# Weaving the fourth retention head with the last delta-rule pair in a two-layer encoder trunk

## The chip, the cores and the metric

The kernel runs on one core of one Trainium2 chip. The metric is the device time of one launch in microseconds (us). The core has a matrix engine (PE, whose weight loads are listed apart as PEld), a vector engine (DVE), a scalar engine (ACT), GpSimd (POOL) and a queue engine that issues the DMAs (SP).

## What is computed

Sixteen learned tokens and 512 input tokens (528 rows of 1024) pass two layers. Each layer adds a token mixer and then a gated feed-forward block; a last norm follows, and the 16 tokens are dropped. The token mixer has two branches that read the same normed input:

```python
o_a = o_fwd + o_bwd            # gated delta rule, 8 heads of 128, both directions
o_a = rms(o_a) * gdn_gain * silu(z_a);  y_a = o_a @ w_up_a
o_b = rms(r_fwd + r_bwd)       # retention, 4 heads, keys of 256, values of 512
o_b = o_b * silu(g_b);          y_b = o_b @ w_up_b
merged = sigmoid(gate_a) * y_a + sigmoid(gate_b) * y_b
return merged @ w_out
```

The delta rule runs chunk by chunk: in each chunk of 128 tokens a triangular system is solved, and a state of 128 x 128 is carried from chunk to chunk. Retention has no state here: scores of all token pairs are formed and weighted by a decay.

## The kernel before

Activations lie transposed, 128 channels by 528 tokens. Products that need fp32 accuracy are made of three passes: a weight tile is split into a high and a low part (`whi`, cast on ACT, L178; `wlo`, on DVE, L179), the activations likewise (`xh`, `xl`), and each of the 8 steps of the contraction issues three matmuls (`mmps`). One projection of 128 output channels is a **unit**. In layer 0 a unit is two halves of 264 tokens, 48 matmuls; in the last layer only 512 tokens are needed for most outputs, and a unit is 24 matmuls of 512 columns, but units for keys and values keep 48. A unit's raw weights (512 KB) come by one DMA into one of three buffers, the split parts into four.

In each layer the eight delta-rule heads run as four pairs (`gi` 0 to 3). `gdn_begin` projects a pair. `gdn_chain` is the long dependent part: products, a solve of about 30 dependent DVE steps that goes out to DRAM (`xd`) and comes back, two rounds of block levels (matmuls `lvy`, `lvt`, `lvq`, `l`, `l64b`), a scan of five chunk steps (matmuls `ks`, `yy`, `sn`, `oo`), and `gdn_squares`, which writes the pair's output to DRAM (`od_a`) and appends a mean-square job to the list `later`. A job in `later` is issued by the next call of `sums`: small matmuls (`oms`), an ACT copy (`ms`) and a DMA to `msd`.

`retention(h)` is a generator over the work of one retention head: two units for queries, two for keys, the rotation, a call of `sums`, the units that were handed in as `filler`, five score blocks (`rs`, evacuated to `pr`) with the units of values 0 and gates 0 among them, and then a loop over four value tiles: values (`dv`), `weighted` (matmuls `rpv`), gates. `filling` chains retention heads 0 to 2, the z gates and the merge gates up to 13.

`weave(a, na, b, nb)` sets the program order. Every generator yields an estimated cost; the loop advances `b` (the filling) and lets `a` (the chain) keep up in the ratio na to nb, until `b` has yielded nb in sum or is empty; then it issues the rest of `a` in one go. The constants are `NA` 71 and `NB` 86. The yields of a whole chain add up to 85.95 in layer 0 and 83.05 in the last layer, so about 15 units of cost at the end of each chain are issued in one go. In the last pair the filling is empty sooner: adding up the yields by hand, the weave ends with the chain at 53.85, in the levels of the second head, and its remaining 32 (29 in the last layer), the whole scan among them, follow in one go. Then comes `retention(3)` with merge gates 14 and 15, by itself, and a last `sums`.

The program order is a priority and not the order of execution. A planner orders the instructions of each engine ahead of the run: it takes the first instruction whose inputs and buffers it expects to be ready, so later work may be pulled forward. PSUM tiles of projections, score blocks and `oms` of these calls share one tag of four buffers; most temporary tiles share a tag of six.

After the mixer, `load_a` (issued with a high priority) turns the eight mean squares into inverse roots (`ir`), reads back the eight delta outputs and z gates (`lo`, `lz`, `rs`), and makes split tiles (`oh`, `ol`) for the projection with `w_up_a`. `load_b` does so for retention, ahead of `w_up_b`.

Of the kernel before, what the change touches and what calls it, by code (L numbers as in the profile page):

```python
# [33 lines left out]
SW = L + 400  # L34
NA = 71.0
NB = 86.0
GF = 2
G0 = 3
HW = 2
# [360 lines left out]
def layer(tc, nc, env, l, xn, gd):  # L400
# [233 lines left out]
    def gdn_decayed(h, st):  # L634

        s = st[h]
        for d in range(2):
            gr = s["gr"][d]
            act(gr, gr, AF.Exp)
            tt(gr, gr, s["q"], MUL)  # L640
        act(s["q"][:, t0:L], s["q"][:, t0:L], AF.Square)
        for c in range(NCH):
            n = tok(c)[1]
            vt = s["vtok"][0:n, c]
            act(vt, vt, AF.Copy, scale=st["nk"][0:n, c, h % 2:h % 2 + 1])
        yield 2.2

    def gdn_solve(st):
        w0 = st["w0"]
        w3 = w0.rearrange("p (r i) -> p r i", r=32)  # L650
        nc.gpsimd.memset(w0[:, 0:1024:33], 1.0)
        for q in range(30, 0, -1):
            n = 31 - q
            t = gp.tile([68, 256], F32, name="st", tag="sc", bufs=SB)[:, :q * n].rearrange("p (j i) -> p j i", j=q)
            tt(t, bc(w3[:, 0:q, q:q + 1], [68, q, n]), bc(w3[:, q:q + 1, q + 1:32], [68, q, n]), MUL)
            tt(w3[:, 0:q, q + 1:32], w3[:, 0:q, q + 1:32], t, ADD)
            if q % 2:
                yield 1.05
        xd = dp.tile([68, 1024], F32, name="xd", tag="xd", bufs=2)
        nc.sync.dma_start(xd, w0)  # L660
        st["xd"] = xd
        yield 4.0
# [181 lines left out]
    def gdn_squares(h, st):  # L844

        s = st[h]
        (o, om), q = s["o"], s["q"]
        o = o.rearrange("p c d -> p (c d)")
        nc.sync.dma_start(od_a[h, :, NM:L], o)
        sq = s["k"]  # L850
        act(sq[:, NM:L], o, AF.Square)
        if not last:
            nc.sync.dma_start(od_a[h, :, 0:NM], om)
            act(sq[:, 0:NM], om, AF.Square)
        stt(sq[:, t0:L], q[:, t0:L], 128.0 * 128.0 * EPS, sq[:, t0:L], MUL, ADD)
        hi, lo = (gp.tile([P, L], F32R, name=n, tag="gcr", bufs=4) for n in ("osh", "osl"))
        split(hi[:, t0:L], lo[:, t0:L], sq[:, t0:L])
        later.append(lambda ps: mean_square(h, (hi, lo), 4.0 / 128.0, 4 * 128 * EPS * 4 * EPS, tmp("ms"), ps))
        yield 1.0
# [3 lines left out]
    def sums(ps):  # L863

        while later:
            later.pop(0)(ps)
# [28 lines left out]
    def gdn_chain(gi, st):  # L895
        hs = (2 * gi, 2 * gi + 1)

        nk = gp.tile([P, NCH, 2], F32, name="nk", tag="nk")
        ssv = st["ssk"].rearrange("p h c -> p c h")
        rk = gp.tile([P, NCH, 2], F32, name="rk", tag="rk")  # L900
        ts(rk, ssv, 4 * EPS, ADD)
        rv, nv = (t.rearrange("p c h -> p (c h)") for t in (rk, nk))
        stt(nv, inverse_root(rv, 2 * NCH), 0.5, rv, MUL, MUL)
        nc.vector.reciprocal(rk, rk)
        cc = gp.tile([P, 2, NCH, 2], F32, name="cc", tag="cc")
        cs = gp.tile([P, 2, NCH, 2], F32, name="cs", tag="cs")
        for d in range(2):
            tt(cc[:, d], beta[:, d, :, 2 * gi:2 * gi + 2], rk, MUL)
            tt(cs[:, d], cc[:, d], sS[:, d, :, 2 * gi:2 * gi + 2], MUL)
        cn = gp.tile([P, 2, NCH, 2], F32, name="cn", tag="cn")  # L910
        ts(cn, cc, -1.0, MUL)
        st.update(nk=nk, cc=cc, cs=cs, cn=cn)
        yield 1.0
        for h in hs:
            yield from gdn_products(h, st)
        for h in hs:
            yield from gdn_decayed(h, st)
        yield from gdn_solve(st)
        for h in hs:
            yield from gdn_levels(h, st)  # L920
        yield from gdn_scan(hs, st)
        for h in hs:
            yield from gdn_squares(h, st)
# [9 lines left out]
    def retention(h, filler):  # L933
# [54 lines left out]
        def values(dv):  # L988
            V[dv] = tmp("rvc")

            def consume(t, n0, n, ps):
                nc.scalar.copy(V[dv][:, n0:n0 + n], ps)
            yield from units(W, C_VB + h * DV + dv * P, 1, xn, FULL, consume)

        def gates(dv):
            G[dv] = tmp("rg")
            yield from units(W, C_GB + h * DV + dv * P, 1, xn, tail, gated(G[dv]))

        def turn(dv):

            vc = V[dv]
            rv = rp.tile([P, 2, NC * P], F32R, name="rv", tag="rot", bufs=2)
            vh, vl = rv[:, 0], rv[:, 1]
            vst = vsts[dv % 2]
            ps = pt("rvt")
            for c in range(NC):
                n0, n = tok(c)
                nc.tensor.transpose(ps[:, c * P:(c + 1) * P], vc[:, n0:n0 + n], ident)
            split(vh, vl, ps)
            pm = pt("rvm")  # L1010
            nc.tensor.transpose(pm[0:NM, 0:P], vc[:, 0:NM], ident)
            split(vst[0:NM], vst[64:64 + NM], pm[0:NM, 0:P])
            nc.scalar.copy(vst[32:32 + NM], vst[0:NM].bitcast(F32))
            V[dv] = vh, vl, vst

        def weighted(dv):
            vh, vl, vst = V[dv]
            o = tmp("ro")
            sq = tmp("rsq2") if S else rp.tile([P, SW], F32, name="rsq", tag="strip")[:, 0:L]
            S.append(sq)  # L1020
            for n0, n in tail:
                ps = pt("rpv")
                for c in range(NC):
                    for a, b in ((vh, 0), (vh, 1), (vl, 0)):
                        mm(ps[:, :n], a[:, c * P:(c + 1) * P], pr[c][b][:, n0:n0 + n], start=c + b == 0 and a is vh, stop=False)
                mm(ps[:, :n], vst, pst[:, n0:n0 + n], start=False)
                act(sq[:, n0:n0 + n], ps[:, :n], AF.Square)
                tt(o[:, n0:n0 + n], ps[:, :n], G[dv][:, n0:n0 + n], MUL)
            nc.sync.dma_start(od_b[h * 4 + dv, :, t0:L], o[:, t0:L])
            if dv:  # L1030
                tt(S[0][:, t0:L], S[0][:, t0:L], sq[:, t0:L], ADD)
# [10 lines left out]
        for dv in range(1, 5):  # L1042
            if dv < 4:
                yield from values(dv)
            weighted(dv - 1)
            yield 3.2
            if dv < 4:
                turn(dv)
                yield from gates(dv)
# [4 lines left out]
    def merge_gates(i0, i1):  # L1054

        for i in range(i0, i1):
            th = tmp("mg")

            def consume(t, n0, n, ps):
                act(th[:, n0:n0 + n], ps, AF.Tanh, scale=0.5)  # L1060
            yield from units(W, C_GA + i * P, 1, xn, tail, consume)
            nc.sync.dma_start(gd[i, :, t0:L], th[:, t0:L])

    def units(src, c0, nt, xs, halves, consume):
        for t in range(nt):
            project(src, c0 + t * P, 1, xs, halves, lambda _, n0, n, ps: consume(t, n0, n, ps))
            yield 5.4

    def z_gates(h0, h1):
        for h in range(h0, h1):  # L1070
            z = tmp("z")
            yield from units(W, C_Z + h * P, 1, xn, tail, gated(z))
            nc.sync.dma_start(zd[h, :, t0:L], z[:, t0:L])

    def weave(a, na, b, nb):

        i = j = 0.0
        while j < nb:
            y = next(b, None)
            if y is None:  # L1080
                break
            j += y
            while a is not None and i * nb < j * na:
                x = next(a, None)
                if x is None:
                    a = None
                    break
                i += x
        for x in a or ():
            i += x  # L1090

    def filling():
        for h in range(3):
            yield from retention(h, z_gates(2 * h, 2 * h + 2))
        yield from z_gates(6, 8)
        yield from merge_gates(G0 + 3 * GF, 14)

    fill = filling()
    for gi in range(4):
        st = {}  # L1100
        extra = merge_gates(G0 + GF * (gi - 1), G0 + GF * gi if gi else 0)
        weave(gdn_begin(gi, st), 32.0, extra, GF * 5.4)
        for _ in extra:
            pass
        weave(gdn_chain(gi, st), NA, fill, NB)
    for _ in fill:
        pass
    for _ in retention(3, merge_gates(14, 16)):
        pass
    sums(pt)  # L1110
    mixctx.close()
# [169 lines left out]
    x2, _ = boundary(nrm, hs, lambda xs, two, **kw: first_units([gate(0), up(0), gate(1)], xs, two, **kw))  # L1281
# [88 lines left out]
```

## Time and profile before

| | us |
|---|---|
| median of 3 runs | 2922.13 |
| lowest and highest | 2919.28, 2929.7 |
| profiled execution, its time | 2919.6 |
| span of its trace | 2917.7 |
| PE busy | 2822.1 (97% of the span) |
| DVE busy | 1795.2 (62%) |
| ACT busy | 1101.0 (38%) |
| chain that ended last: PE, DVE, DMA | 84%, 8%, 5% |

Layer 0 fills the first half of the span and layer 1, the last, the second. The part that the change touches, from the last pair's levels to the start of the projection with `w_up_a`, lies between 762 and 907 us and between 2205 and 2351 us. In a table of windows, busy time is summed for each engine, and "PEclk" is the mean granted clock of PE as a share of 2.4 GHz. A matmul whose line ends in brackets was preceded by PE idle time, and the brackets say how long and which instruction ended it.

### The profile page before, as it was taken

Reading aid. Unit: us, or ns where it says so; the run is one execution under the profiler, and the core shown is the slowest. Engines: PE = TensorE matmul, PEld = TensorE weight load, DVE = VectorE, ACT = ScalarE, POOL = GpSimd, SP = SyncE. Lnnn points to the kernel's source line nnn. Section 1 sums busy time; section 2 is a strip of 40 time slices with the busy share of each in tenths; the row PEclk is TensorE's granted clock in tenths of the full one; section 3 lists DMA queues with packets and bytes.
Section 4 is the critical chain, followed back from the end, with each engine's and each line's share of the span. In section 5 each row is a group of like instructions: output and inputs, shape, how many; then the busy total and the mean of one; then the engine's idle time right before and its main releaser. Section 6 shows DMA issues by size and latency. Waiting matters only on the chain.

```text
span 2917.7 us, 48775 instructions
## 1 busy us (share of the span) xinstructions
PE 2822.1 (97%) x19487; PEld 2579.0 (88%) x19487; DVE 1795.2 (62%) x3854; ACT 1101.0 (38%) x2171; POOL 9.0 (0%) x114
## 2 busy tenths in 40 slices
PE   8999999999999999999999999999997999999998
PEld 8999999999889999999999888888886788888887
DVE  6877858768664545343258779687786564543433
ACT  5444445345333233222234344453443332332222
POOL 0000000000000000000000000000000000000000
PEclk9999999999899999999999999999998999999999
DMA  5433323324245442333444423334241464433332
GB/s 166 112 83 83 100 77 85 99 74 125 70 145 171 137 143 84 91 89 99 123 116 112 107 71 108 88 94 106 71 140 44 154 192 125 130 109 94 92 110 80
DMA packets 506423, 313.48 MB, mean 107 GB/s; under 512 B 55633, under 2 KB 460779, under 8 KB 506195
## 3 DMA queue, kind: packets, MB, share of 16 engines
q1 hardware_dynamic: 506194, 310.36, 37.1%
q8 instruction: 153, 2.51, 0.4%
q14 instruction: 76, 0.61, 0.1%
HBM read 265.28 MB, written 45.02 MB: 106 GB/s over the span
## 4 chain that ended last, share of the span: by engine, by line
PE 84%; DVE 8%; DMA 5%; ACT 2%; issue 1%; SPq 0%; DVEq 0%; ACTq 0%
PE mmps L112 67%; PE rpv L112 3%; PE fu L112 2%; PE oo L112 2%; PE sn L112 1%; DVE wlo L179 1%; PE yy L112 1%; DMA xd<-w 1%; PE ks L112 1%; DMA lo<-od_a 1%; PE rs L112 1%; PE lvy L112 1%; PE lvt L112 1%; DMA lo<-od_b 1%; PE lvq L112 1%
## 5 line engine op out<-in xcount | busy, mean ns | idle before, releaser
L112 PE MATMUL mmps<-xh,whi 128*128 128x264 f32 (+1 forms) x3840 | 1188.0, 310 | 23.7 <-DVE rg L115 12.4
L112 PE MATMUL mmps<-xl,whi 128*128 128x264 f32 (+1 forms) x3840 | 1179.5, 308 | 0.0
L112 PE MATMUL mmps<-xh,wlo 128*128 128x264 f32 (+1 forms) x3808 | 1173.3, 308 | 0.0
L112 PEld LDWEIGHTS mmps<-xh,whi 128*128 128x128 f32 x3840 | 727.2, 189 | 63.2 <-DVE rg L115 14.6
L178 ACT CAST whi<-wraw 128x1024 fp32r<-128x1024 f32 (+1 forms) x392 | 407.3, 1040 | 991.2 <-PE mmps L112 737.0
L179 DVE TENSOR_TENSOR wlo<-wraw,whi 128x1024 fp32r<-128x1024 f32 (+1 forms) x392 | 474.4, 1210 | 485.3 <-ACT whi L178 484.4
L112 PEld LDWEIGHTS mmps<-xl,whi 128*128 128x128 f32 x3840 | 726.2, 189 | 37.0 <-issue 2.9
L112 PEld LDWEIGHTS mmps<-xh,wlo 128*128 128x128 f32 x3808 | 719.9, 189 | 34.3 <-issue 0.5
L112 PE MATMUL mmps<-oh,whi 128*128 128x264 f32 (+2 forms) x1126 | 358.5, 319 | 0.0
L112 PE MATMUL mmps<-oh,wlo 128*128 128x264 f32 (+2 forms) x1126 | 358.1, 318 | 0.0
L112 PE MATMUL mmps<-ol,whi 128*128 128x264 f32 (+2 forms) x1126 | 357.3, 318 | 0.5 <-DVE ol L179 0.4
L112 PEld LDWEIGHTS mmps<-ol,whi 128*128 128x128 f32 x1126 | 211.6, 188 | 16.4 <-DVE ol L179 0.9
L112 PEld LDWEIGHTS mmps<-oh,wlo 128*128 128x128 f32 x1126 | 211.7, 188 | 15.7 <-issue 0.2
L112 PEld LDWEIGHTS mmps<-oh,whi 128*128 128x128 f32 x1126 | 211.5, 188 | 15.0
L115 DVE SCALAR_TENSOR_TENSOR ac<-xc,cw,ac 128x528 f32<-128x528 f32 x192 | 143.6, 759 | 3.4 <-ACT ac L125 0.6
L118 DVE TENSOR_TENSOR ff<-fg,mmps 128x264 f32<-128x264 f32 (+1 forms) x63 | 32.5, 516 | 116.0 <-PE mmps L112 116.0
L112 PE MATMUL rpv<-prh,rv 128*128 128x264 f32 (+1 forms) x384 | 95.5, 323 | 0.0
L118 DVE TENSOR_TENSOR st<-w 68x30 f32<-68x30 f32 (+14 forms) x240 | 78.2, 326 | 19.0 <-DMA w<-ndm 7.1
L118 DVE TENSOR_TENSOR w<-w,st 68x30 f32<-68x30 f32 (+14 forms) x240 | 78.2, 326 | 6.8
L125 ACT ACTIVATE gth<-mmps 128x264 f32<-128x264 f32 (+1 forms) x132 | 59.8, 454 | 57.4 <-PE mmps L112 57.4
L112 PE MATMUL rs<-rot 128*128 128x264 f32 (+3 forms) x240 | 75.1, 456 | 2.8 <-DVE z L115 2.4
L115 DVE SCALAR_TENSOR_TENSOR hn<-mmps,hold 128x264 f32<-128x264 f32 (+2 forms) x51 | 25.4, 498 | 82.6 <-PE mmps L112 76.5
(315 smaller groups left out, 3216.3 us busy)
## 6 DMA issues: line engine op xcount, KB each, us to landing
wraw<-in_w_in_dram SPq DMA_DIRECT2D x194, 512.0 KB
wraw<-in_w_ffn_in_dram SPq DMA_DIRECT2D x88, 512.0 KB
wraw<-in_w_up_b_dram SPq DMA_DIRECT2D x32, 512.0 KB
wraw<-in_w_ffn_out_dram SPq DMA_DIRECT2D x32, 512.0 KB
gcr<-grow SPq DMA_DIRECT2D x32, 264.0 KB
wraw<-in_w_up_a_dram SPq DMA_DIRECT2D x16, 512.0 KB
wraw<-in_w_out_dram SPq DMA_DIRECT2D x16, 512.0 KB
wraw<-in_w_ffn_out_dram SPq DMA_DIRECT2D x16, 384.0 KB
```

What stands on the lines that cost most here:

```text
L112: newest[0] = nc.tensor.matmul(o, lhsT=l, rhs=r, start=start, stop=stop)
L115: (eng or nc.vector).scalar_tensor_tensor(out=o, in0=a, scalar=s, in1=b, op0=op0, op1=op1)
L118: (eng or nc.vector).tensor_tensor(out=o, in0=a, in1=b, op=op)
L125: nc.scalar.activation(o, a, f, **kw)
L178: a = nc.scalar.copy(hi, src)
L179: return a.ins, nc.vector.tensor_tensor(out=lo, in0=src, in1=hi.bitcast(F32), op=SUB).ins
```

## The change

The last pair's chain is woven up to 86 instead of 71, with the filling up to 86 x 86 / 71 = 104.2, so the ratio of the two stays. `retention(3)` with merge gates 14 and 15 becomes the end of `filling` instead of a loop of its own after it. And in the loop over value tiles of `retention`, `sums` is called after the values are projected, ahead of `weighted`.

```diff
 NA = 71.0
 NB = 86.0
+NZ = 86.0
...
         for dv in range(1, 5):
             if dv < 4:
                 yield from values(dv)
+            sums(pt)
             weighted(dv - 1)
...
         yield from merge_gates(G0 + 3 * GF, 14)
+        yield from retention(3, merge_gates(14, 16))
...
-        weave(gdn_chain(gi, st), NA, fill, NB)
+        weave(gdn_chain(gi, st), *((NA, fill, NB) if gi < 3 else (NZ, fill, NZ * NB / NA)))
     for _ in fill:
-        pass
-    for _ in retention(3, merge_gates(14, 16)):
         pass
     sums(pt)
```

## Rows read from the trace of the kernel before

**Rows 1.** Head of the page: busy us, share of span, instructions

```profile
PE 2822.1 (97%) x19487; PEld 2579.0 (88%) x19487; DVE 1795.2 (62%) x3854; ACT 1101.0 (38%) x2171; POOL 9.0 (0%) x114
```

**Rows 2.** Windows, layer 1: stretch, length, busy by engine, PEclk, DMA share, GB/s

```profile
2205.00:2215.00 10.00, 0.00 (x0) 0.00 (x0) 5.98 (x13) 4.57 (x14) 0.00 (x0) 0.74 0.36 80
2215.00:2225.00 10.00, 8.71 (x56) 7.76 (x56) 3.24 (x9) 2.29 (x9) 0.00 (x0) 0.57 0.12 22
2225.00:2235.00 10.00, 6.29 (x40) 5.87 (x40) 4.62 (x12) 3.08 (x11) 0.00 (x0) 0.66 0.01 2
...
2257.00:2267.00 10.00, 7.57 (x29) 5.54 (x28) 3.26 (x7) 2.56 (x5) 0.00 (x0) 0.83 0.14 54
...
2294.00:2306.00 12.00, 7.80 (x52) 7.48 (x52) 9.91 (x17) 4.38 (x9) 0.00 (x0) 0.86 0.76 231
...
2205.00:2351.00 146.00, 123.77 (x712) 103.75 (x713) 78.79 (x164) 51.40 (x119) 0.00 (x0) 0.91 0.32 96
```

**Rows 3.** Windows of the same kind, layer 0

```profile
775.00:785.00 10.00, 8.66 (x58) 7.75 (x58) 2.94 (x8) 1.50 (x5) 0.00 (x0) 0.60 0.01 2
785.00:796.00 11.00, 11.00 (x61) 9.99 (x60) 6.41 (x20) 4.25 (x15) 0.00 (x0) 0.69 0.01 1
...
811.00:821.00 10.00, 7.25 (x38) 6.20 (x37) 3.02 (x6) 3.24 (x9) 0.00 (x0) 0.66 0.16 54
...
842.00:862.00 20.00, 16.15 (x115) 13.91 (x116) 18.06 (x30) 9.04 (x18) 0.00 (x0) 1.00 0.87 266
...
762.00:907.00 145.00, 131.83 (x972) 122.46 (x973) 83.85 (x183) 53.70 (x130) 0.00 (x0) 0.92 0.34 101
```

**Rows 4.** Timeline of PE, layer 1: start, us, engine, line, tiles, shape, count

```profile
2204.59 0.39 PE L112 MATMUL oms<-prl,one 128*1 128x512 f32 x1
2215.39 2.08 PE L112 MATMUL lvy<-QT,N 128*128 128x128 f32 x8 [10.42 <-DVE QT L118]
...
2256.96 0.65 PE L112 MATMUL oo<-P,xx 128*128 128x128 f32 x4
...
2260.66 0.39 PE L112 MATMUL mmps<-xh,whi 128*128 128x512 f32 x1
```

**Rows 5.** Timeline of DVE, layer 1, the last weight split before the scan

```profile
2205.51 1.23 DVE L179 TENSOR_TENSOR wlo<-wraw,whi 128x1024 fp32r<-128x1024 f32 x1 [2.96 <-ACT whi L178]
```

**Rows 6.** Timeline of PE, layer 0, around the first level

```profile
763.02 1.16 PE L112 MATMUL lvy<-QT,N 128*128 128x128 f32 x8 [1.43 <-DVE QT L118]
763.93 0.37 PE L112 MATMUL mmps<-xh,whi 128*128 128x264 f32 x1
```

**Rows 7.** Sums of windows over levels and scans, woven pairs, layers 0 and 1

```profile
sum 229.00, PE 224.94 PEld 212.89 DVE 143.33 ACT 92.67 POOL 1.23; mean PE 24.99 PEld 23.65 DVE 15.93 ACT 10.30 POOL 0.14
...
sum 131.50, PE 129.48 PEld 120.46 DVE 86.02 ACT 55.25 POOL 0.77; mean PE 21.58 PEld 20.08 DVE 14.34 ACT 9.21 POOL 0.13
```

**Rows 8.** Timelines, both layers: last oms of the pair, last ol of load_a

```profile
819.84 0.64 PE L112 MATMUL oms<-osl,one 128*1 128x264 f32 x2
...
864.42 0.70 DVE L179 TENSOR_TENSOR ol<-lo,oh 128x528 fp32r<-128x528 f32 x1
...
2266.86 0.39 PE L112 MATMUL oms<-osl,one 128*1 128x512 f32 x1
...
2308.60 0.69 DVE L179 TENSOR_TENSOR ol<-lo,oh 128x512 fp32r<-128x512 f32 x1
```

**Rows 9.** Chain that ended last, both layers: start, us, engine, tile, line, count

```profile
861.98 3.16 PE rpv L112 x26
...
903.95 3.17 PE rpv L112 x26
...
2306.46 3.02 PE rpv L112 x13
...
2342.30 5.57 PE mmps L112 x24
2347.86 3.00 PE rpv L112 x13
```

## The prediction

> **What bounds the kernel now.** I read the page's head first: PE is busy for 97% of the span [rows 1], and no other engine comes near. So only two things can move the time much: PE work that goes away, and PE time in which nothing, or only half as much, is done. The change removes no matmul, so I went on to tables of windows over each layer and looked for stretches where PE busy falls or the granted clock does. Outside the start and the ends of the layers they sit in one place per layer, around the levels and scan of the last pair. In layer 1 PE does nothing at all from 2205 to 2215, and then runs at a mean granted clock of 0.57 and 0.66 for 20 us, between its levels of 1.2 and 2.4 GHz [rows 2]; layer 0 has the same picture, milder [rows 3]. The timeline tells why. The last matmul before the hole ends at 2205.0, and PE stands 10.42 us until the solved blocks come (`lvy`) [rows 4]. Yet the split weights of the next units were there: the last `wlo` before the scan ends at 2206.7 [rows 5], four sets are buffered, and no unit runs until 2260.66, right behind the scan's last `oo` at 2257.6 and the first `oms` [rows 4]. What holds the units is program order: in `retention(3)` the call of `sums` stands ahead of merge gates 14 and 15, it holds the mean squares of the last pair, which wait for the end of the scan, and the units behind it take PSUM tiles of the same tag. That the planner serves a tag in program order is my reading of these rows; it isn't written in the kernel.
>
> **What the lost time is worth.** Idle time is the window less PE busy: 146 - 123.77 = 22.2 us in layer 1 [rows 2] and 145 - 131.83 = 13.2 us in layer 0 [rows 3]. To it comes busy time at a low clock, which I price at busy x (1 - clock). Layer 1: 8.71 x 0.43 + 6.29 x 0.34 + 7.57 x 0.17 + 7.80 x 0.14 = 8.3 us [rows 2]. Layer 0: 8.66 x 0.40 + 11.00 x 0.31 + 7.25 x 0.34 = 9.3 us [rows 3]. Together 53.0 us. The Trainium skill (Perfetto Trace Analysis, Identifying the Most-Contended Engine) warns that matmul busy time is a bad measure and asks for the weight loads' busy time instead. By that the loss would be 146 - 103.75 and 145 - 122.46, together 64.8 us [rows 2, 3]. I don't take it: of the woven stretches in layer 1, where PE has next to no idle time, weight loads fill only 120.46 of 131.5 us [rows 7]; and at the low clock both measures look full, as between 785 and 796 us, where only the clock shows the loss [rows 3].
>
> **The change, part by part.**
> *Order of the last pair.* With the same ratio, nothing moves until the filling is empty, at cost 53.85 of the chain. From there two units of queries and two of keys, merge gates 14 and 15, score blocks 0 and 1 and values 0 come between the rest of the levels and the scan. Those four first units ran before the levels already, in the solve's shadow; what is new is all that stood behind `sums`. That call now finds only the job of retention 2. So merge gates 14 and 15, five score blocks, values 0, gates 0 and values 1 may run as soon as their inputs are there: six units and scores, over 30 us of PE work (a unit is 5.57 us [rows 9]). The holes before the scan's end are smaller than that. For the 10.42 us hole, two units with weights in place make 11.1 us.
> Does the planner see the hole? It can only fill what its own clock shows. In layer 0 it put `lvy` ahead of the last matmuls of the keys, and PE then waited 1.43 us [rows 6]. So its clock for the solve's end was early by about that. I take 1.4 us as the part of a hole it would miss.
> *What stays.* In the other five pairs, where filling was at hand, levels and scan left 229 - 224.94 = 4.1 us idle in three pairs of layer 0 and 131.5 - 129.48 = 2.0 us in the two pairs of layer 1 that I summed [rows 7], so 1.4 and 1.0 us a pair, 2.4 us in both layers. Then the stalls while `load_a` runs: 12 - 7.80 = 4.2 us idle and 1.1 us of low clock in layer 1 [rows 2], 20 - 16.15 = 3.9 us in layer 0 [rows 3]. `load_a` is not removed, it only meets another part of the retention, so I keep them: 9.2 us (bounds 0 to 18: gone, or doubled).
> *The new call of sums.* For pairs 0 to 2 and in the earlier heads `later` is empty there, so it issues nothing. In the last pair it issues the two mean squares, ahead of `weighted(0)`. On PE's queue all of `weighted` and what follows stands behind these `oms`; they wait for the scan's end. In a dense order the scan ends some 20 us before PE has done the work that stands ahead of them, so I cost this wait at nothing. If the chain ran longer than that, PE would stand.
> *DMAs and the other engines.* The moved head issues twelve weight loads of 512 KB on SP, two gate stores, four output stores and one decay strip. They pass the two or four output stores of the pair and its small reads of `xd`. Buffered weights for four units (22 us) cover the time that SP waits for the solve's blocks; if the cover failed, the bound is the 10.42 us hole again. On DVE and ACT the evacuations of scores, values and gates, and a weight split of 1.23 us [rows 5] per unit, now come between the steps of the scan. That makes the chain longer, by between 0 and some 10 us (eight such splits), but PE is what is full there, and this is free so long as `oms` isn't late.
> *What is late next.* `load_a` needs all eight mean squares. From the last `oms` to its last `ol` it took 2309.3 - 2267.3 = 42.0 us in layer 1 and 865.1 - 820.5 = 44.6 in layer 0 [rows 8]. Before, `oms` had nearly the whole head behind it as cover. Now the cover is what follows values 1: from the first `rpv` to the end of the last, 2350.9 - 2306.5 = 44.4 us and 907.1 - 862.0 = 45.1 us [rows 9]. The first unit with `w_up_a` reads the eighth head last, some 4.9 us (7/8 of 5.57) after it starts. So the slack is 44.4 + 4.9 - 42.0 = 7.3 us in layer 1 and 45.1 + 4.9 - 44.6 = 5.4 us in layer 0. It just fits.
>
> **Sum.** 53.0 - 2.4 - 9.2 = 41.4 us: 24.2 in layer 1 (30.5 less 1.0 and 5.3), 17.2 in layer 0 (22.5 less 1.4 and 3.9). The profiled execution took 2919.6 us, so it would take 2878.2. It lies 2.5 us under the median of the runs, and against the median I forecast 2922.1 - 41.4 = **2881 us**. With the bounds of the kept stalls and 1.4 us missed per hole this case spans 2868 to 2893.
>
> **The rivals.**
> *load_a becomes the bound.* Its DVE work now runs against the loop over value tiles, and DVE is an in-order queue that was nearly full while it ran (18.06 of 20 us [rows 3], 9.91 of 12 [rows 2]). If it takes a third longer, or the chain ends as much later, layer 1 loses 14.0 - 7.3 = 6.7 us and layer 0 14.9 - 5.4 = 9.5. With some 4 us of low clock behind such holes the gain is 21 us: **2901**. For it: the slack is thin. Against: the loop loads DVE less than the scores did.
> *The holes stay.* The planner thinks the solve is done sooner than it is, and queues the new work behind `lvy`. Then the 10.42 us hole [rows 4] and the low clock behind it (5.9 us in layer 1 [rows 2]), 1.4 us [rows 6] and 6.9 us in layer 0 [rows 3] remain: 24.6 us less, **2905**. Against it stands the 1.43 us of layer 0, which shows the planner's clock to be nearly right.
> *The clock.* Small matmuls between units leave short gaps, and the clock could swing. The Trainium skill (TensorE: Matmul & The Clock Gate, A second HAM failure mode: psum-queue depth-cycling) says that many micro-idles between groups of matmuls do that. If the stretch from the first level to `oms` (about 67 and 80 us) ran at a mean of 0.75, midway between the levels, it would lose a quarter, some 37 us: **2918**. Against: the woven pairs lost only 1.0 to 1.4 us of idle time each [rows 7], so there are few gaps.
> *Slower.* The same `load_a`, but much later: it needs its inverse roots through DRAM and 24 reads of tiles, and the loop's evacuations and weight splits stand with it on DVE and SP. If it took twice as long, PE would wait 42.0 - 7.3 = 34.7 us in layer 1 and 44.6 - 5.4 = 39.2 in layer 0, and 73.9 - 41.4 = 32.5 us would be lost: **2955**. It decides at (41.4 + 7.3 + 5.4) / 86.6 = 0.62, so from 1.6 times its present length on. Nothing in the rows points to that.
>
> **How the numbers follow.** Forecast 0.64, load_a the bound 0.18, holes stay 0.08, clock 0.05, slower 0.05. About 0.5% (14.6 us) is what a measurement of this kernel can tell from no change. Faster by more: the forecast, the first rival and half of the second (2905 lies at the edge of 2907.5), 0.86. Within: the other half and the clock, 0.09. Slower: 0.05. The range must leave out no more than 2 in 10: the forecast's own 2868 to 2893, widened to the first rival, gives 2866 to 2903.
>
> **What would show it.** Right: `mmps` between 2205 and 2215 and between `lvy` and `lvt`; a granted clock near 1.00 through the last pair; `oms` of the last pair some 20 to 30 us later than before and behind a unit of values; the first `w_up_a` unit some 24 us earlier in layer 1 than 2351. Wrong: `lvy` still waiting 10 us with nothing ahead; a wait of PE for `ol` or `oh` at the first `w_up_a` unit, which means `load_a` ends late; `oms` waiting for `osh`, which means the chain ends late; or units behind `sums` that start only after `oms`, which means the buffers' order wasn't what held them.

## The result and the profile after

The changed kernel takes 2885.28 us (median of 4 runs, 2884.81 to 2888.39); beside it the kernel before took 2925.91 (2919.28 to 2931.21). The ratio is 0.986, with a 95% interval of 0.985 to 0.987: some 40 us less, where 41.4 were forecast; the forecast of 2881 us lies 4 us below the median. The profiled executions lie 34.9 us apart in span (2917.7 and 2882.8), and it is this difference that the parts below add up to. The head of the page of after, which answers [rows 1]:

```profile
span 2882.8 us, 48770 instructions
PE 2809.8 (97%) x19487; PEld 2567.1 (89%) x19487; DVE 1795.3 (62%) x3854; ACT 1099.1 (38%) x2171; POOL 8.9 (0%) x114
```

The instructions are the same in number, on every engine. PE is busy for 12.3 us less (2822.1 - 2809.8); no matmul is gone, and more of them ran at the full clock. The rest of the 34.9, 22.6 us, is idle time that went. Windows of after, with the columns of [rows 2]; the first six are layer 1, the last three layer 0:

```profile
2200.00:2210.00 10.00, 10.00 (x50) 7.39 (x50) 8.58 (x16) 6.31 (x14) 0.00 (x0) 1.00 0.70 188
2210.00:2220.00 10.00, 10.00 (x86) 8.25 (x85) 6.13 (x15) 5.92 (x19) 0.00 (x0) 1.00 0.18 37
2220.00:2230.00 10.00, 10.00 (x44) 6.43 (x44) 5.21 (x8) 3.10 (x6) 0.00 (x0) 1.00 0.22 54
2260.00:2275.00 15.00, 11.63 (x56) 8.85 (x55) 6.78 (x17) 4.85 (x10) 0.00 (x0) 0.89 0.15 54
2275.00:2315.00 40.00, 40.00 (x225) 34.69 (x224) 27.01 (x47) 13.78 (x26) 0.00 (x0) 1.00 0.75 225
2192.00:2315.00 123.00, 118.69 (x721) 98.27 (x719) 75.32 (x161) 49.28 (x116) 0.00 (x0) 0.99 0.40 114
...
820.00:850.00 30.00, 26.03 (x193) 23.32 (x192) 18.36 (x56) 10.28 (x29) 0.00 (x0) 0.94 0.14 46
860.00:870.00 10.00, 7.78 (x51) 7.25 (x50) 8.44 (x14) 4.89 (x11) 0.00 (x0) 0.83 1.07 338
759.00:894.00 135.00, 128.06 (x994) 119.22 (x993) 84.59 (x184) 53.35 (x132) 0.00 (x0) 0.97 0.37 110
```

Where layer 1 had an empty stretch of 10 us and 20 us at a clock of 0.57 to 0.66 [rows 2], PE is now busy without a gap at 1.00. What remains is one thin place per layer, at the end of the scan (2260 to 2275 and 820 to 850), and in layer 0 the stall while `load_a` runs (860 to 870). Lost time by the same count as in the prediction: layer 1, 123 - 118.69 = 4.3 us idle and 118.69 x 0.01 = 1.2 us of low clock; layer 0, 135 - 128.06 = 6.9 us idle and 128.06 x 0.03 = 3.8 us.

The timeline of PE in layer 1, after: first the place of the hole in [rows 4], then the end of the scan (start, length, engine, line, tiles, shape, count, and in brackets the idle time before):

```profile
2203.52 1.02 PE L113 MATMUL rs<-rot 128*128 128x512 f32 x2
2204.38 1.05 PE L113 MATMUL lvy<-QT,N 128*128 128x128 f32 x8
2205.27 2.74 PE L113 MATMUL rs<-rot 128*128 128x512 f32 x6
2207.44 0.69 PE L113 MATMUL mmps<-xh,whi 128*128 128x264 f32 x1
...
2209.68 1.05 PE L113 MATMUL lvt<-Y,QT 128*128 128x128 f32 x8
...
2262.43 0.65 PE L113 MATMUL oo<-P,xx 128*128 128x128 f32 x4
2265.24 0.40 PE L113 MATMUL oms<-osh,one 128*1 128x512 f32 x1 [2.16 <-ACT osh L179]
2265.90 0.39 PE L113 MATMUL oms<-osh,one 128*1 128x512 f32 x1 [0.26 <-ACT osh L179]
2266.12 0.40 PE L113 MATMUL rpv<-prh,rv 128*128 128x512 f32 x1
```

`lvy` waits for nothing any more: two units of 24 matmuls ran ahead of it, from 2192.43 on, and score blocks and matmuls of a unit stand between the levels. At the end of the scan, though, `oms` still waits 2.16 us for its input, now with the score products (`rpv`) queued behind it. The kernel before had the same wait at the same place:

```profile
2259.77 0.39 PE L112 MATMUL oms<-osh,one 128*1 128x512 f32 x1 [2.16 <-ACT osh L178]
```

The waits of PE from there to the start of the next stage, layer 0 and then layer 1 (engine, tile, line, what it waited for: us in total, times, longest):

```profile
PE oms L113 <- ACT osh L179: 2.4, 2, 1.3
PE mmps L113 <- DVE ro L119: 1.8, 1, 1.8
PE sn L113 <- DVE xx L123: 1.2, 1, 1.2
```

```profile
PE oms L113 <- ACT osh L179: 2.4, 2, 2.2
PE rvm L1012 <- ACT ms L126: 0.7, 1, 0.7
PE oo L113 <- DVE xx L123: 0.7, 1, 0.7
PE mmps L113 <- DVE wlo L180: 0.3, 1, 0.3
```

No wait for `oh` or `ol` is among them: PE never stands for a tile of `load_a`. The 1.8 us of layer 0 are a wait for DVE, which has `load_a` to do in that stretch (8.44 of 10 us busy from 860 to 870), to take a result of `weighted` out of its buffer (`ro`).

The projection with `w_up_a` doesn't begin behind the whole head, neither before nor after. In layer 1 its first ten matmuls, on the first heads of `load_a`, stand ahead of the head's last unit and of the last `rpv`, which ends at 2350.9 us before and at 2314.5 after. The first of the ten, before and after:

```profile
2339.40 0.48 PE L112 MATMUL mmps<-oh,whi 128*128 128x512 f32 x1
...
2302.14 0.48 PE L113 MATMUL mmps<-oh,whi 128*128 128x512 f32 x1
```

By parts of the span: in layer 0 from the end of the last matmul ahead of the last pair's first level to the end of the last `rpv`, 145.5 us shrink to 133.9 (11.6); in layer 1 from the start of the last `oms` of retention 2, 146.5 shrink to 122.6 (23.9). All else together is 0.6 us longer. 11.6 + 23.9 - 0.6 = 34.9.

### The profile page after: what moved, and what is told of

Read it like the earlier page. It is cut to its first block, busy times and chain, and to the rows that moved or that the text cites. A ratio compares the mean times of both kernels' runs of the same rounds, so it can differ in the third digit from the quotient of the medians.

```text
span 2882.8 us, 48770 instructions
## 1 busy us (share of the span) xinstructions
PE 2809.8 (97%) x19487; PEld 2567.1 (89%) x19487; DVE 1795.3 (62%) x3854; ACT 1099.1 (38%) x2171; POOL 8.9 (0%) x114
## 4 chain that ended last, share of the span: by engine, by line
PE 87%; DVE 6%; DMA 4%; ACT 1%; issue 1%; SPq 0%; DVEq 0%; ACTq 0%
PE mmps L113 69%; PE rpv L113 3%; PE fu L113 3%; PE oo L113 2%; PE rs L113 1%; PE sn L113 1%; PE yy L113 1%; DMA xd<-w 1%; DVE wlo L180 1%; PE ks L113 1%; PE l L113 1%; PE l64b L113 1%; DMA lo<-od_b 1%; PE kk L113 1%; ACT whi L179 1%
## 5 line engine op out<-in xcount | busy, mean ns | idle before, releaser
L113 PEld LDWEIGHTS mmps<-xh,whi 128*128 128x128 f32 x3840 | 726.5, 189 | 57.5 <-DVE rg L116 8.5
```

The lines of the kernel that those rows point to most:

```text
L113: newest[0] = nc.tensor.matmul(o, lhsT=l, rhs=r, start=start, stop=stop)
```

## The experiments

Two theories went into the runs. **A**: what counts is the place at which the mean squares of the last pair are issued, because what stands behind them in the same buffer tag is held by them. **B**: what counts is that the fourth head is woven with the chain.

**Either part alone.** The first run takes from the changed kernel the new call of `sums` and leaves the weave. The second does the reverse: the kernel before, with `retention(3)` left behind the weave, and only the mean squares of the last pair moved behind values 1.

```diff
 # e1_no_call, against the changed kernel
             if dv < 4:
                 yield from values(dv)
-            sums(pt)
             weighted(dv - 1)
```

> The changed kernel without the call of sums in the loop over value tiles; nothing is left out of the computation. Theory A, the call's place is what counts: with no call in the loop, the whole fourth head runs before the scan's end, the last pair's mean squares come after it, and load_a, 42 to 45 us, has no cover: some 35 to 40 us lost in each layer, so 2885 + 75 = about 2960 us, slower than before. Theory B, the weave with the fourth head brings the gain and the call only helps: a few us of cover lost in each layer, 2890 to 2900 us.

```diff
 # e2_sums_only, against the kernel before
-        sums(pt)
+        if h < 3:
+            sums(pt)
+        else:
+            later.pop(0)(pt)
...
                 yield from values(dv)
+            if h == 3:
+                sums(pt)
```

> The kernel before, with the fourth head in its old place behind the last pair, and only the last pair's two mean squares moved behind values 1 (retention 2's stays). Theory A: the gain is all there, 2885 us, ratio 0.986. Theory B: without the weave nothing is gained, 2922 us, ratio 1.00.

The weave without the call gave 2920.07 us, ratio 0.999 (0.997 to 1.000): no difference that can be told. The moved mean squares without the weave gave 2885.85, ratio 0.987 (0.985 to 0.989): the whole gain. More than that, its instructions stand in the same order on every engine as the changed kernel's. The new constant, the ratio and the head's move into `filling` therefore change nothing by themselves; they act only in that `sums` in `retention(3)` now runs before the last pair has put its jobs on the list. Theory A held, B fell. Windows of e2, where [rows 2] show the hole:

```profile
2205.00:2215.00 10.00, 10.00 (x78) 8.36 (x78) 5.25 (x10) 3.34 (x10) 0.00 (x0) 1.00 0.60 160
2215.00:2225.00 10.00, 10.00 (x61) 7.17 (x60) 7.87 (x16) 5.67 (x16) 0.00 (x0) 1.00 0.21 54
2225.00:2235.00 10.00, 10.00 (x66) 7.51 (x65) 5.54 (x10) 4.89 (x11) 0.00 (x0) 1.00 0.18 52
```

In e1 the hole is gone too, but the time is lost later. There the whole fourth head is done before the last `oms` of the pair (in layer 1 even before the scan ends), and nothing is left to cover `load_a`. Waits of PE in e1, layer 0 and layer 1, and its timeline in layer 1:

```profile
PE mmps L113 <- ACT oh L179: 14.9, 1, 14.9
...
PE mmps L113 <- ACT oh L179: 17.0, 2, 16.0
...
2317.44 1.06 PE L113 MATMUL oms<-osl,one 128*1 128x512 f32 x2
2334.52 2.08 PE L113 MATMUL mmps<-oh,whi 128*128 128x512 f32 x4 [16.02 <-ACT oh L179]
```

After the last `oms` PE stands for 16.02 us, until the first split tile of `load_a` is there. That is not the 42 us that `load_a` takes to its last tile [rows 8]: the unit begins with the first head and follows the others as they come. So the call in the loop is what keeps part of the head behind `oms` as cover; it is no detail of the change but, by e2, enough for all of it.

**Do buffers hold the units?** If the units wait behind the mean squares because of a shared tag, a tag of their own must fill the hole, with the call where it was. The first try gave all delta pairs' mean squares another tag, the second only the last pair's.

```diff
 # e5_other_tags, against the kernel before
-        later.append(lambda ps: mean_square(h, (hi, lo), 4.0 / 128.0, 4 * 128 * EPS * 4 * EPS, tmp("ms"), ps))
+        later.append(lambda ps: mean_square(h, (hi, lo), 4.0 / 128.0, 4 * 128 * EPS * 4 * EPS, ctmp("ms"), ct))
```

> The kernel before, with sums where it was, but the delta heads' mean squares take their PSUM tiles and their row tiles from the other two tags, so that merge gates 14 and 15 and what follows no longer stand behind them for a buffer. Theory A: PE no longer idles 10 us ahead of the first level of layer 1, but as nothing holds the fourth head it is all done by the scan's end and load_a is uncovered: about 2950 to 2960 us. If it wasn't the buffers that held the units: the hole of 10 us stays and the time is as before, 2922 us.

```diff
 # e5b_tags_last_pair, against the kernel before
-        later.append(lambda ps: mean_square(h, (hi, lo), 4.0 / 128.0, 4 * 128 * EPS * 4 * EPS, tmp("ms"), ps))
+        later.append(lambda ps: mean_square(h, (hi, lo), 4.0 / 128.0, 4 * 128 * EPS * 4 * EPS, (ctmp if h > 5 else tmp)("ms"), ct if h > 5 else ps))
```

> The kernel before, with sums where it was; only the last pair's two mean squares take their PSUM and row tiles from the other two tags. Theory A, the units behind sums were held by those tiles: PE no longer idles 10 us ahead of layer 1's first level, and the fourth head runs before the scan's end; load_a is uncovered as in the kernel without the call, so about 2920 us with a wait of some 15 us for oh in each layer. If the tiles didn't hold them: the 10 us hole stays, 2922 us, and no wait for oh.

Both edits move two tiles at once, the PSUM tile and the row tile (`ms`), each out of a tag that it shares with the units into one that it shares with the chains. The first settles little: 2947.41 us, ratio 1.008 (1.006 to 1.010). The earlier pairs lost time in the chains' tags: from the products (`kk`) of the first pair to those of the last, layer 1 took 569 us instead of 542. The hole itself was gone (in the whole run no `lvy` waited longer than 3.5 us). The second is clean: 2913.35 us, ratio 0.996 (0.995 to 0.998). Waits of PE in layer 1, and then in layer 0:

```profile
PE mmps L112 <- ACT oh L178: 15.1, 1, 15.1
...
PE oms L112 <- ACT prh L178: 5.6, 1, 5.6
PE lvy L112 <- DVE QT L118: 0.5, 1, 0.5
```

Layer 1 has no wait of `lvy` left and layer 0 one of 0.5 us, though no call was moved: it was a shared tag that held the units. Which of the two tags did is not shown. In layer 1 the gain then goes the way it went in e1, into a wait of 15.1 us for `oh`, since the whole head runs ahead of the scan's end. In layer 0, where the same was expected, there is no wait for `oh`: 12.6 us of the head were left behind the last `oms`, and the longest wait is 5.6 us, for retention's own mean squares. The Trainium skill (Perfetto Trace Analysis, Optimization Strategy) says that the same gap, coming back on the engine that should be full, can mean that a pool lacks buffers for the next tile. The gap of this case comes once in a layer and not as a series. The rows of e5b agree that buffers held PE, with the 10.42 us of [rows 4] down to none; those of e2 show that a call put elsewhere frees them without any more buffers, and is worth 37 us (1.3%) where the other tag is worth 11.

**Where the call should stand.** The same call, one place earlier and one or two later:

```diff
 # e10_sums_earlier, against the changed kernel
             if dv < 4:
+                sums(pt)
                 yield from values(dv)
-            sums(pt)
...
 # e6_sums_later, against the changed kernel
-            sums(pt)
+            if dv > 1:
+                sums(pt)
...
 # e13_sums_latest, against the changed kernel
-            sums(pt)
+            if dv > 2:
+                sums(pt)
```

> The changed kernel with the call of sums one unit earlier, ahead of values 1. Theory A: 5.8 us less of the head may run before the scan's end, so the scan ends up to 5 us sooner but PE runs dry sooner too: 5 us more idle in each layer, about 2893 us; load_a has 5.8 us more cover and needs none of it. If load_a were the bound in the changed kernel: 2875 us.

> The changed kernel with the call of sums one value tile later, ahead of weighted(1). Theory A: 15 us more of the head may run before the scan's end, which fills most of the 11 us (layer 0) and 6 us (layer 1) still lost there, but the cover of load_a falls from 45 to 30 us against 43 to 45 needed, less the 5 us of the first unit: some 8 to 10 us of waiting with low clock behind it in each layer. Net 2885 to 2900 us. If load_a had slack to spare: 2870 us.

> The changed kernel with the call of sums two value tiles later, ahead of weighted(2). All of PE's idle time at the scan's end is filled, and load_a's cover is 15 us. If load_a decided by its last head, as the prediction had it: 25 us lost in each layer less some 8 gained, about 2920 us. If what must be covered is the way to its first head, about 16 us: little lost, 2885 to 2895 us.

| call stands ahead of | last `oms` to end of last `rpv`, layers 0 and 1 (us) | median (us) | ratio (95%) |
|---|---|---|---|
| values 1 (e10) | 57.5, 50.1 | 2887.73 | 0.986 (0.985 to 0.988) |
| `weighted(0)` (the change) | 48.3, 42.8 | 2885.28 | 0.986 (0.985 to 0.987) |
| `weighted(1)` (e6) | 28.7, 25.7 | 2883.99 | 0.985 (0.983 to 0.987) |
| `weighted(2)` (e13) | 12.9, 9.8 | 2903.20 | 0.992 (0.991 to 0.994) |
| nothing, all is done (e1) | -1.1, -10.5 | 2920.07 | 0.999 (0.997 to 1.000) |

The second column is the work that covers `load_a`; matmuls with `w_up_a` that run ahead of the last `rpv` are counted in it. One unit earlier (e10) makes no difference that can be told. With 26 us of cover (e6) there is still no loss, where 8 to 10 us of waiting in each layer were expected and the prediction had held 44 against 42 for a close fit; PE waits 1.5 us in all for `oh` and `ol`. Nor is there a gain: `oms` waits 2.4 us for `osh` in each layer, as in the changed kernel, so what the later call lets through runs ahead of that wait and not in it. With 10 to 13 us (e13) the kernel loses 18 us against the change, between the two cases of its expectation, and with none 35. Of those 18 in e13 the windows from 759 to 920 and from 2192 to 2350 show about 10 as more idle time: 21.3 us against 11.5 in the changed kernel. Its waits there, in layer 0 and in layer 1:

```profile
PE oms L113 <- ACT prh L179: 5.6, 1, 5.6
PE mmps L113 <- ACT whi L179: 2.1, 1, 2.1
...
PE oms L113 <- DVE prl L180: 2.9, 1, 2.9
PE oms L113 <- ACT prh L179: 2.7, 1, 2.7
```

These are the mean squares of retention: PE has run out of other work and reaches them before their input. So between some 26 and 57 us of cover there is a broad flat place, and the change sits on it.

**Is `load_a` near the edge?** Three kernels load it differently: its inverse roots in two parts, so that the first six heads need not wait for the last pair; the same together with the later call; and all its reads of outputs and gates done twice.

```diff
 # e8_split_roots, against the changed kernel
-        inverse_roots(0, 8)
+        inverse_roots(0, 6)
+        inverse_roots(6, 2)
...
 # e9_split_later and e14_split_later_again: e8 and e6 together
...
 # e11_load_twice, against the changed kernel
-            nc.sync.dma_start(o[:, t0:L], od_a[h, :, t0:L])
-            nc.sync.dma_start(z[:, t0:L], zd[h, :, t0:L])
+            for _ in range(2):
+                nc.sync.dma_start(o[:, t0:L], od_a[h, :, t0:L])
+                nc.sync.dma_start(z[:, t0:L], zd[h, :, t0:L])
```

> The changed kernel with the inverse roots of the first six delta heads taken in a call of their own, which needn't wait for the last pair. If load_a is covered in the changed kernel, as theory A has it, this changes nothing: 2885 us. If load_a's length is paid for: up to 10 us less per layer, 2870 us.

> The changed kernel with both: sums one value tile later and the first six heads' roots in a call of their own, so that load_a starts some 10 us sooner. Theory A: the shorter cover of 30 us is then nearly enough, and the 17 us still lost at the scan's end are mostly filled: 2872 to 2880 us, below the changed kernel. If it is not the cover that the later call costs: the same time as with the later call alone.

> The version with the call one value tile later and the first six heads' roots apart, the fastest so far, once more with more rounds. If it is faster than the changed kernel (ratio 0.9859 to the kernel before): 0.984 or less with an interval that stays below 0.9859. If not: a ratio within 0.001 of 0.9859.

> The changed kernel with load_a reading each head's output and z gate twice (4 MB more per layer). If the slack is as thin as forecast (5 to 7 us, eight heads needed by the end of the first unit): load_a gets some 15 us longer, 8 to 10 us lost in each layer, 2905 us. If, as the kernel without the call suggests, the first unit keeps pace with the heads as they come and the slack is wide: no more than 5 us in each layer, 2885 to 2895 us.

Splitting the roots gave 2888.42 us, ratio 0.986 (0.984 to 0.988): nothing. Both edits together gave 2882.03, 0.984 (0.983 to 0.986), and in five more rounds 2881.25, 0.986 (0.984 to 0.988): not to be told from the change. A `load_a` that starts earlier is worth nothing, then; it is covered. With all its reads doubled the time is 2898.54 us, ratio 0.991 (0.990 to 0.993), 13 us more than the change over two layers (16 by the ratios), between the two cases of its expectation. The last `ol` of `load_a` lands 62.5 and 60.3 us behind the last `oms`, where it was 43.3 and 44.6 in the changed kernel. The waits of PE up to 960 us in layer 0 and up to 2420 in layer 1:

```profile
PE mmps L113 <- ACT oh L179: 3.9, 3, 1.7
PE mmps L113 <- DVE ol L180: 2.9, 5, 1.2
...
PE mmps L113 <- DVE ol L180: 2.1, 3, 1.2
PE mmps L113 <- DVE wlo L180: 1.6, 1, 1.6
PE mmps L113 <- ACT oh L179: 1.4, 2, 1.2
```

Together 11.9 us, where the changed kernel has 0.8. By the times of the single waits, 4.7 of them are for heads of `load_a`, six waits of 1.7 us or less: PE takes the heads one by one and waits a little for some. Another 5.5 come later (952 to 956 and 2374 to 2386), for the first tiles of `load_b`, which stands behind `load_a`, and 1.6 are for a weight split. So of the 16 to 19 us by which `load_a` is longer, 3.3 us in layer 0 and 1.4 in layer 1 come out as waits for its heads; the rest was slack or is paid for behind it.

**Does the low clock come from the hole?** The prediction counted 5.9 us of low clock in layer 1 as what the hole leaves behind. This run fills the hole with 36 products per layer that nobody uses, and leaves everything else as before.

```diff
 # e7_warm_hole, against the kernel before
         nc.sync.dma_start(xd, w0)
         st["xd"] = xd
+        if st.get("gi") == 3:
+            wm = ct("wm")
+            for _ in range(36):
+                mm(wm[:, 0:P], w0[0:64, 0:P], ident[0:64, :])
```

> The kernel before, with 36 small matmuls more per layer that read the solved blocks and that nobody uses, so that PE has work in the 10 us ahead of the last pair's first level. If the low clock behind the hole is what makes the levels slow: granted clock near 1.00 and some 5 to 6 us less between the first lvy and the last l64b of layer 1 (21.3 us before), and about 2916 us in all. If the levels are slow by their own waits: 21 us as before and no gain.

It took 2924.29 us, ratio 1.000 (0.999 to 1.001). Timeline and windows of PE in layer 1:

```profile
2205.40 8.30 PE L112 MATMUL wm<-c_ident,w 64*128 64x128 f32 x72
2216.25 1.16 PE L112 MATMUL lvy<-QT,N 128*128 128x128 f32 x8 [2.54 <-DVE QT L118]
2218.19 2.08 PE L112 MATMUL lvt<-Y,QT 128*128 128x128 f32 x8 [0.78 <-DVE Y L118]
```

```profile
2205.00:2215.00 10.00, 8.71 (x75) 8.11 (x72) 5.12 (x11) 4.80 (x14) 0.00 (x0) 1.00 0.29 58
2216.00:2226.00 10.00, 8.32 (x56) 7.55 (x56) 3.38 (x9) 3.25 (x12) 0.00 (x0) 0.58 0.08 14
2226.00:2237.00 11.00, 7.37 (x52) 6.72 (x53) 4.83 (x14) 3.10 (x11) 0.00 (x0) 0.61 0.01 1
```

Of the hole 8.3 us are filled, at 1.00, and 2.54 are left ahead of `lvy`; the levels behind it still run at 0.58 and 0.61, as they did behind an empty hole (0.57 and 0.66 [rows 2]). From the first `lvy` to the last `l64b` it takes 21.2 us, where it took 21.3. So in layer 1 the levels, run alone, are slow without a hole of 10 us as well; a run without the last 2.54 us was not made, so that the gap has no part in it is not shown. In layer 0 the added products shifted the order, units came between the levels and the clock there was 1.00 from 765 to 785; the head still ended at 908.0 us there, against 907.1 before. Here filling the gap with empty work was worth nothing; filling it with units that must run anyhow, as in e2, is what saved.

## Why the prediction was right, and where its terms were off

**What bounds, and why the units stood still: right.** PE was the bound, the loss lay around the levels and scan of the last pair, and the units were held by program order in a shared tag. The prediction called the last a reading of rows; e2 and e5b show it, but for which of two shared tags it was. That the hole and the low clock go was right too: `lvy` waits for nothing in layer 1, and the three windows there stand at 1.00.

**Which line does it: half said.** The prediction saw that `sums` in `retention(3)` finds only the job of retention 2, but wrote the weave as the cause and the new call as a price of nothing. By e1 and e2 it is the reverse: the weave matters only through that empty list, and without the call the gain is gone.

**Layer 1: 24.2 forecast, 23.9 measured, by two errors that cancel.** Kept were 1.0 us of the weave's residue and 5.3 us of `load_a`'s stalls. The stalls did not come: PE is full from 2275 to 2315, and the one wait near there is 0.3 us. Instead 4.3 us idle and 1.2 us of low clock stand at the end of the scan, 5.5 in all for the 6.3 that were kept. By this count 25.0 us would have come back, so 1.1 us stay unaccounted for. That forecast and measurement come out alike is luck.

**Layer 0: 17.2 forecast, 11.6 measured.** The same stretch of `load_a` cost 2.2 us idle and 7.78 x 0.17 = 1.3 us of low clock, close to the 3.9 that were kept. The missing 5.6 us are the end of the scan: from 820 to 850 4.0 us idle and 26.03 x 0.06 = 1.6 us of low clock.

**The step that failed, in both layers.** It is the wait at the end of the scan: "the scan ends some 20 us before PE has done the work that stands ahead of them, so I cost this wait at nothing". The 20 us have no working behind them (and the six units counted there are five: merge gates 14 and 15, values 0 and 1, gates 0). In the trace that work was done at 822 and at 2242 us, and the scan ended at 837.3 and 2263.1, so 15 and 21 us after it, not 20 before. The planner ran the units as soon as they were ready and let the scan's steps come between. Seen from the pair's last products ahead of the solve (`km`), the scan ended after 141.9 us in layer 0 (114.0 before) and 131.0 us in layer 1 (113.1). Its last steps ran bare (three in layer 0, four in layer 1), and `oms` waited up to 1.3 and 2.2 us with the rest of the head queued behind it. The prediction had named this sign: "`oms` waiting for `osh`, which means the chain ends late". It had put the longer chain at 0 to 10 us and free; it was 28 and 18 us longer. What was lost by this is not a new cost but a saving that did not come: the sum counts the end of the scan as recovered, 2.75 + 2.5 = 5.2 us in layer 0 (811 to 821 [rows 3]) and 2.4 + 1.3 = 3.7 in layer 1 (2257 to 2267 [rows 2]), and after the change it costs 5.6 and 5.5, with the same waits for `osh`.

**`load_a`: right that it isn't the bound, wrong on how close.** The prediction held cover and need as 44.4 + 4.9 against 42.0 us and called it a close fit. Its length was judged well (44.6 us after in layer 1 and 43.3 in layer 0, from `oms` to the last `ol`). But it had the first unit with `w_up_a` begin behind the last `rpv`, and in the kernel before its first matmuls already ran 11.5 us ahead of that (2339.40 against 2350.9); by its own sum the cover would then have been too short. And the need was not all eight heads at the end of the first unit: in e6 some 26 us of cover do as well as 43. So the fit was neither as close as the sum says nor for the reason it gives. That `load_a` isn't the bound came out right; the sum of cover and need doesn't show why. The price of the rival with a chance of 0.18 was too high: in e11 `load_a` is 16 to 19 us longer and 13 to 16 us are lost in both layers together, where the rival set some 20 for 14 to 15. But as e1 shows, with no cover at all the whole gain goes.

**The other rivals.** The holes did not stay, and `load_a` did not take twice as long. The clock did not swing in the woven stretch, which ran at 1.00 from 2200 to 2230 with PE busy for all of it. The Trainium skill (TensorE: Matmul & The Clock Gate, A second HAM failure mode: psum-queue depth-cycling) tells of a kernel whose clock swings because PE stands idle briefly and often between groups of matmuls. The three windows show no such idle time and no such loss.

**The signs.** `oms` came 25 us later in layer 0 (838.6 to 845.2, [rows 8]). In layer 1 it is 5 us later on the trace, where all ahead had moved up by 12.4 us, so some 17, a little less than the 20 to 30 foreseen. The last `rpv` ends at 2314.5 us, 36.3 earlier than 2350.9 [rows 9], of which 12.4 come from layer 0 and the stages between; the rest is 23.9. The first matmul with `w_up_a` is 37.3 us earlier, 24.9 by the same count, where 24 were foreseen.

**The size.** Against the medians (2925.91 to 2885.28) the saving is 40.6 us, near the 41.4. The trace that the sum was made from lies 6 us under the median of before in that set, and on the traces the saving is 34.9. So the sum was 6.5 us too high for the profiled execution: 5.6 in layer 0, 0.3 in layer 1 and 0.6 elsewhere. That the medians agree within 1 us is luck: the four runs of the kernel before spread over 12 us, and the sum is read from the trace of one of the fastest. The lower end of the prediction's own span, 2868, doesn't follow from the bounds it names: with none of the kept stalls the sum gives 2871.5, and with nothing kept at all 2869.

## What to carry to other kernels

When PE stands although weights and inputs of later units are there, look for an instruction ahead of them in program order that takes a buffer of the same tag and waits for something late; moving that one call can be worth as much as rewriting the order around it. But what is freed runs at once, so check what is then left to cover the next dependent stage: here some 26 us of work behind the mean squares did, 10 to 13 us did not. Before a larger edit is credited, its parts should be run one by one, since one of two parts here was without any effect by itself.

## What the runs showed of the hardware that was not expected

In layer 1 of e7 PE ran at a granted clock of 1.00 (2.4 GHz) without a gap until 2213.7 us, stood for 2.54 us, and ran the first level's `lvy` in 1.16 us. After another 0.78 us of standing the same shape (`lvt`) took 2.08, and the clock was at the lower level:

```profile
2218.00:2220.00 2.00, 1.81 (x8) 1.81 (x9) 0.13 (x1) 0.00 (x0) 0.00 (x0) 0.50 0.00 0
```

With units between them in the changed kernel the same levels ran at 1.00. Scan steps that run bare, one close behind the other, ran at 1.00 in layer 1: 18.58 us busy of 19 in the kernel before, and 16.06 of 17 in the changed one:

```profile
2237.00:2256.00 19.00, 18.58 (x143) 16.98 (x143) 14.28 (x51) 7.01 (x24) 0.00 (x0) 1.00 0.00 1
```

```profile
2243.00:2260.00 17.00, 16.06 (x125) 14.89 (x124) 13.46 (x45) 5.94 (x22) 0.00 (x0) 1.00 0.11 31
```

In layer 0 of the kernel before they did not: from 785 to 796 PE is busy for all 11.00 us with the first scan steps, and the mean clock is 0.69 [rows 3]. So in these rows the clock fell without a gap of 10 us, and a busy PE was no sign of a full clock; what decides between the two scans isn't shown.
